# Sliding windows on one Trainium2 core: three DMA rings in place of two, other packet sizes, a last store in parts

## Chip, cores and metric

The kernel runs on one core of a Trainium2 chip. The metric is device time in microseconds; lower is better. The kernel before takes 763.64 us (median of three runs, 762.43 to 763.97).

## What is computed

For each of 32 batches of 4096 rows by 256 float32, the 127 windows of 64 rows that start every 32 rows are copied out:

```python
n_windows = (length - window_size) // stride + 1      # (4096 - 64) // 32 + 1 = 127
for i in range(n_windows):
    start = i * stride
    result[:, i] = x[:, start:start + window_size].copy()
```

Nothing is calculated. The input is 134 MB, the output 266 MB: each row, but for the first and last 32 of a batch, is written twice.

## The kernel before

Thirty-two rows of a batch are one block: 128 blocks of 32 KB in a batch. Window w is blocks w and w + 1, 64 KB, contiguous in input and output. There are two ways to make a batch's output.

A *copied* batch goes from HBM to HBM (`copy`, L93): 127 rows of 64 KB, in three DMAs of 80, 32 and 15 rows. `COPY_PARTS` (L16) gives in how many parts a row is cut, so the packets are 16, 32 and 16 KB. SP issues these DMAs. A DMA spreads its outermost rows evenly over up to 16 DMA engines; the 15-row DMA uses 15.

A *staged* batch is read once and written twice. `load` (L75) brings it to an SBUF tile, one block to each of the 128 partitions; `store` (L83) writes the tile to the output two times, shifted by half a window: `half` 0 makes block j the first half of window j, `half` -1 the second half of window j - 1. Both are issued by ACT in packets of 16 KB (`2 * BLOCK_PARTS`, so 65536 / 4 bytes). There is no window 127, and none before window 0, so a store also writes one block into the first half-window of the next batch and one into the last half-window of the batch before. Whatever writes those two batches must come later, or must be mended.

The 12 odd batches 1 to 23 are staged (`STAGED`), through five tiles (`BUFS`). The other 20 are copied. Their order is made by `_order` (L102): first the four batches of `EARLY`, 18, 20, 22 and 24, then batch 25, and then the batches 26 to 31 between those that touch a staged batch ("tied": 0, 2, ..., 16). Counted from 0, the tied batches stand at places 5, 6, 8, 10, 11, 13, 15, 16 and 18 of the 20, and each waits on SP for the stores of its staged neighbours (L134 to L137); the later of those is store 0 for batch 0, store 1 for batch 2, up to store 8 for batch 16. The `EARLY` batches don't wait: they are written before the stores of their neighbours (ACT waits for them once, L146), and the seven half-windows that those stores then spoil are written again at the end (L151 to L158) by small DMAs of 32 KB in 2 KB packets, each behind its store.

ACT's own order is load 0, load 1, store 0, load 2, store 1, and so on. A load into a tile that has been used waits for that tile's store (L79), a store waits for its load (L88). At the end SP waits for all stores and copies and clears the 12 semaphores one by one (L159 to L163).

All bytes thus go through two queues: q1, SP's, with 166.5 MB of copies, and q10, ACT's, with 50.3 MB of loads and 100.7 MB of stores. DMA engines take packets from the queues that have some.

Of the kernel before, what the change touches and what calls it, by code (L numbers as in the profile page):

```python
# [1 line left out]

# [4 lines left out]


STAGED = tuple(range(1, 24, 2))
BUFS = 5  # L10

EARLY = (18, 20, 22, 24)

BLOCK_PARTS = 2

COPY_PARTS = ((80, 4), (32, 2), (15, 4))  # L16


class _Geometry:


    def __init__(self, x, out, W, S):
        self.B, self.L, self.D = x.shape
        self.x, self.out = x, out
        self.n_win = (self.L - W) // S + 1
        self.n_blk = self.L // S
        self.blk = S * self.D
        self.win = W * self.D
        assert W == 2 * S and self.n_blk == self.n_win + 1 == 128

    def src(self, b, block, dims):

        at = (b * self.n_blk + block) * self.blk
        return bass.AP(self.x.tensor, self.x.offset + at, dims)

    def dst(self, b, half, dims):

        at = b * self.n_win * self.win + half * self.blk
        return bass.AP(self.out.tensor, self.out.offset + at, dims)

    def rows(self, b, w0, n):

        s, d = [[self.blk, n], [1, self.win]], [[self.win, n], [1, self.win]]
        return self.dst(b, 2 * w0, d), self.src(b, w0, s)

    def half(self, b, half, block):

        dims = [[self.blk // 16, 16], [1, self.blk // 16]]
        return self.dst(b, half, dims), self.src(b, block, dims)


class _Kernel:
    def __init__(self, nc, g, tiles):
        self.nc, self.g, self.tiles = nc, g, tiles
        self.loaded = [nc.alloc_semaphore(f"loaded{i}") for i in range(len(tiles))]
        self.stored = [nc.alloc_semaphore(f"stored{i}") for i in range(len(tiles))]
        self.copied = nc.alloc_semaphore("copied")
        self.early = nc.alloc_semaphore("early")
        self.count = {}

    def start(self, engine, out, in_, sem, parts=1):
        engine.dma_start(out=out, in_=in_, max_dma_last_dim=65536 // parts).then_inc(sem, 16)
        self.count[id(sem)] = self.count.get(id(sem), 0) + 16

    def all_of(self, engine, sem):
        engine.wait_ge(sem, self.count[id(sem)])

    def slot(self, n):
        return divmod(n, len(self.tiles))

    def after_store(self, engine, n):
        turn, i = self.slot(n)
        engine.wait_ge(self.stored[i], 32 * (turn + 1))

    def load(self, n):  # L75

        g, (_, i) = self.g, self.slot(n)
        if n >= len(self.tiles):
            self.after_store(self.nc.scalar, n - len(self.tiles))  # L79
        src = g.src(STAGED[n], 0, [[g.blk, g.n_blk], [1, g.blk]])  # L80
        self.start(self.nc.scalar, self.tiles[i][:, :], src, self.loaded[i], 2 * BLOCK_PARTS)

    def store(self, n):  # L83

        g, (turn, i) = self.g, self.slot(n)
        self.nc.scalar.wait_ge(self.loaded[i], 16 * (turn + 1))  # L88
        for half in (0, -1):
            dst = g.dst(STAGED[n], half, [[g.win, g.n_blk], [1, g.blk]])  # L90
            self.start(self.nc.scalar, dst, self.tiles[i][:, :], self.stored[i], 2 * BLOCK_PARTS)

    def copy(self, b, sem):  # L93

        w = 0
        for rows, parts in COPY_PARTS:
            self.start(self.nc.sync, *self.g.rows(b, w, rows), sem, parts)
            w += rows
        assert w == self.g.n_win


def _order(B):  # L102


    near = {b for s in STAGED for b in (s - 1, s + 1)}
    order = list(EARLY) + [b for b in range(B) if b not in near and b not in STAGED]
    tied = sorted(near - set(EARLY))
    n = len(order) + len(tied)
    for b in tied:
        behind = max(STAGED.index(s) for s in (b - 1, b + 1) if s in STAGED)  # L110
        order.insert(-(-(2 * behind + 5) * n // (2 * len(STAGED))), b)
    return order


@with_exitstack
def kernel(
    ctx: ExitStack,
    tc: tile.TileContext,
    x: bass.AP,
    window_size: bass.AP,  # L120
    stride: bass.AP,
    out: bass.AP,
):
    nc = tc.nc
    W, S = int(window_size), int(stride)
    g = _Geometry(x, out, W, S)
    assert 0 not in STAGED and g.B - 1 not in STAGED
    pool = ctx.enter_context(tc.tile_pool(name="blocks", bufs=1))
    tiles = [pool.tile([g.n_blk, g.blk], x.dtype, name=f"xb{i}") for i in range(BUFS)]

    with tc.tile_critical():
        k = _Kernel(nc, g, tiles)
        for b in _order(g.B):
            if b not in EARLY:  # L134
                for s in (b - 1, b + 1):
                    if s in STAGED:
                        k.after_store(nc.sync, STAGED.index(s))  # L137
            k.copy(b, k.early if b in EARLY else k.copied)
        k.load(0)
        waited = False  # L140
        last = len(STAGED) - 1
        for n, s in enumerate(STAGED):
            if n < last:
                k.load(n + 1)
            if not waited and (s - 1 in EARLY or s + 1 in EARLY):
                k.all_of(nc.scalar, k.early)  # L146
                waited = True
            k.store(n)


        k.all_of(nc.sync, k.early)  # L151
        for n, s in enumerate(STAGED):
            if s - 1 in EARLY or s + 1 in EARLY:
                k.after_store(nc.sync, n)
            if s - 1 in EARLY:
                k.start(nc.sync, *g.half(s - 1, 2 * g.n_win - 1, g.n_blk - 1), k.copied)
            if s + 1 in EARLY:
                k.start(nc.sync, *g.half(s + 1, 0, 0), k.copied)  # L158
        for n in range(len(STAGED)):  # L159
            k.after_store(nc.sync, n)  # L160
        k.all_of(nc.sync, k.copied)
        for sem in [*k.loaded, *k.stored, k.copied, k.early]:
            nc.sync.sem_clear(sem)  # L163


# [1 line left out]
_INS = ['x', 'window_size', 'stride']  # L167
_OUTS = [((32, 127, 64, 256), 'float32')]

_NUMBERS = {'window_size': 64, 'stride': 32}  # L170


# [26 lines left out]
```

## Time and profile before

| | |
|---|---|
| median of the runs | 763.64 us |
| the profiled execution | 768.4 us |
| its span, first to last instruction | 766.6 us |
| packets, bytes | 19837, 317.70 MB |
| mean rate | 414 GB/s |
| HBM read, written | 217.02 MB, 267.35 MB |
| first bulk packet, last packet | 2.0 us, 763.8 us |

The program has no compute instruction that matters (four memsets on GpSimd, 0.2 us), so the page's chain of waits and its groups of instructions say nothing. What is left to read is the DMA part: slices of the span with the DMA engines' busy share and their rate, the queues, the list of issues with the time from issue to landing, stretches of time with their rate, and what the queues' own sequencers waited for.

The list of issues has, for each kind, output and input, queue, count, KB each, and the median us from issue to landing:

```profile
out_dram<-in_x_dram SPq DMA_DIRECT2D x20, 5120.0 KB, 114.8
out_dram<-xb ACTq DMA_DIRECT2D x24, 4096.0 KB, 84.6
xb<-in_x_dram ACTq DMA_DIRECT2D x12, 4096.0 KB, 123.2
out_dram<-in_x_dram SPq DMA_DIRECT2D x20, 2048.0 KB, 116.7
out_dram<-in_x_dram SPq DMA_DIRECT2D x20, 960.0 KB, 97.7
out_dram<-in_x_dram SPq DMA_DIRECT2D x7, 32.0 KB, 48.3
```

The first, fourth and fifth rows are the three DMAs of a copy, the sixth the small ones at the end. A DMA lands some 100 us after its issue because it stands in its queue behind others. What SP's sequencer waited for (us in total, times, longest):

```profile
SPq L62 <- DMA out_dram<-xb: 61.2, 2, 40.2
SPq L73 <- DMA out_dram<-xb: 19.2, 3, 9.4
SPq L66 <- DMA out_dram<-in_x_dram: 7.7, 1, 7.7
```

The first two rows are waits for stores, the third is the wait at the end for the last copies. While SP waits, its queue still holds DMAs that were issued before.

### The profile page before, as it was taken

The numbers are of one execution on the slowest core, as the hardware profiler recorded it, in microseconds if no ns is written. First come the engines' busy times: TensorE is split into PE (matmuls) and PEld (weight loads), VectorE is DVE, ScalarE is ACT, GpSimd is POOL, SyncE is SP. The second block draws the span as 40 slices with busy tenths as digits, with TensorE's granted clock in tenths as the row PEclk, the third lists the DMA queues.
The fourth block names the chain that finished last, engine by engine and source line by source line (L and its number), as shares of the span: only waits on it lengthen the run. The fifth ranks groups of instructions, "written<-read, shape, count | busy, mean of one in ns | idle before, by whom it ended". The sixth has DMA issues, their size and how long they took to land. (4 is left out here: it accounts for less than half of the span.)

```text
span 766.6 us, 180 instructions
## 1 busy us (share of the span) xinstructions
POOL 0.2 (0%) x4
## 2 busy tenths in 40 slices
POOL 0000000000000000000000000000000000000000
DMA  8999999999999999999999999999999999999996
GB/s 371 425 410 421 405 428 431 408 411 427 423 415 421 431 415 425 432 408 416 427 420 417 431 420 420 423 428 410 414 427 419 422 428 418 417 428 421 420 406 237
DMA packets 19837, 317.70 MB, mean 414 GB/s; under 512 B 1628, under 2 KB 1628, under 8 KB 1740
## 3 DMA queue, kind: packets, MB, share of 16 engines
q1 hardware_dynamic: 10044, 166.70, 51.9%
q10 hardware_dynamic: 9792, 151.00, 47.3%
q14 instruction: 1, 0.01, 0.0%
HBM read 217.02 MB, written 267.35 MB: 632 GB/s over the span
## 5 line engine op out<-in xcount | busy, mean ns | idle before, releaser
L180 POOL MEMSET const-bfloat16-1.0<- 128x1 bf16 x1 | 0.1, 102 | 0.0
L180 POOL MEMSET const-uint8-127<- 128x1 uint8 x1 | 0.1, 102 | 0.0
L180 POOL MEMSET const-float32-0.0<- 128x1 f32 x1 | 0.1, 99 | 0.2 <-issue 0.2
L180 POOL MEMSET const-float32-1.0<- 128x1 f32 x1 | 0.1, 99 | 0.0
## 6 DMA issues: line engine op xcount, KB each, us to landing
out_dram<-in_x_dram SPq DMA_DIRECT2D x20, 5120.0 KB, 114.8
out_dram<-xb ACTq DMA_DIRECT2D x24, 4096.0 KB, 84.6
xb<-in_x_dram ACTq DMA_DIRECT2D x12, 4096.0 KB, 123.2
out_dram<-in_x_dram SPq DMA_DIRECT2D x20, 2048.0 KB, 116.7
out_dram<-in_x_dram SPq DMA_DIRECT2D x20, 960.0 KB, 97.7
out_dram<-in_x_dram SPq DMA_DIRECT2D x7, 32.0 KB, 48.3
```

What stands on the lines that cost most here:

```text
L180: nc = _bacc.Bacc("TRN2", target_bir_lowering=False, num_devices=1)
```

## The change

- Loads move from ACT to GpSimd and get packets of 8 KB, but for load 0, which stays on ACT, is issued first of all, and has packets of 32 KB and a semaphore of its own. GpSimd issues loads 1 to 11 one after the other, each waiting only for its tile.
- ACT then holds load 0 and the stores, which keep their 16 KB packets.
- A copy's three DMAs have 96, 16 and 15 rows, in packets of 32, 16 and 64 KB.
- The last store (batch 23) is made in three parts of 32, 32 and 64 partitions, each with both halves: first the two outer parts, with a semaphore of their own, then the middle one. The two small DMAs that mend batches 22 and 24 wait for the outer parts alone.
- At the end GpSimd instead of SP waits for all semaphores, resets its DMA queue and clears the semaphores as one range.

The order of the copies, the staged batches, the five tiles and the bytes moved are the same.

```diff
-BLOCK_PARTS = 2
-
-COPY_PARTS = ((80, 4), (32, 2), (15, 4))
+
+LOAD_PACKET = 8192
+STORE_PACKET = 16384
+COPIES = ((96, 2), (16, 4), (15, 1))
+
+
+LAST = ((0, 32), (96, 32), (32, 64))
...
-    def start(self, engine, out, in_, sem, parts=1):
-        engine.dma_start(out=out, in_=in_, max_dma_last_dim=65536 // parts).then_inc(sem, 16)
+    def start(self, engine, out, in_, sem, packet=65536):
+        engine.dma_start(out=out, in_=in_, max_dma_last_dim=packet).then_inc(sem, 16)
...
         if n >= len(self.tiles):
-            self.after_store(self.nc.scalar, n - len(self.tiles))
+            self.after_store(self.nc.gpsimd, n - len(self.tiles))
         src = g.src(STAGED[n], 0, [[g.blk, g.n_blk], [1, g.blk]])
-        self.start(self.nc.scalar, self.tiles[i][:, :], src, self.loaded[i], 2 * BLOCK_PARTS)
-
-    def store(self, n):
+        if n == 0:
+            self.start(self.nc.scalar, self.tiles[i][:, :], src, self.first)
+        else:
+            self.start(self.nc.gpsimd, self.tiles[i][:, :], src, self.loaded[i], LOAD_PACKET)
+
+    def store(self, n, p0, rows, sem=None):
...
         g, (turn, i) = self.g, self.slot(n)
-        self.nc.scalar.wait_ge(self.loaded[i], 16 * (turn + 1))
+        if n == 0:
+            self.all_of(self.nc.scalar, self.first)
+        else:
+            self.nc.scalar.wait_ge(self.loaded[i], 16 * (turn + (i > 0)))
         for half in (0, -1):
-            dst = g.dst(STAGED[n], half, [[g.win, g.n_blk], [1, g.blk]])
-            self.start(self.nc.scalar, dst, self.tiles[i][:, :], self.stored[i], 2 * BLOCK_PARTS)
+            dst = g.dst(STAGED[n], 2 * p0 + half, [[g.win, rows], [1, g.blk]])
+            src = self.tiles[i][p0 : p0 + rows, :]
+            self.start(self.nc.scalar, dst, src, sem or self.stored[i], STORE_PACKET)
...
         w = 0
-        for rows, parts in COPY_PARTS:
-            self.start(self.nc.sync, *self.g.rows(b, w, rows), sem, parts)
-            w += rows
+        for n, parts in COPIES:
+            self.start(self.nc.sync, *self.g.rows(b, w, n), sem, 4 * self.g.win // parts)
+            w += n
...
         k = _Kernel(nc, g, tiles)
+        k.load(0)
         for b in _order(g.B):
...
-        k.load(0)
+        for n in range(1, len(STAGED)):
+            k.load(n)
...
-            if n < last:
-                k.load(n + 1)
             if not waited and (s - 1 in EARLY or s + 1 in EARLY):
                 k.all_of(nc.scalar, k.early)
                 waited = True
-            k.store(n)
+            if n < last:
+                k.store(n, 0, g.n_blk)
+            else:
+                for p0, rows in LAST:
+                    alone = p0 > 0 and p0 + rows < g.n_blk
+                    k.store(n, p0, rows, None if alone else k.fringe)
...
-            if s - 1 in EARLY or s + 1 in EARLY:
+            if n == last:
+                k.all_of(nc.sync, k.fringe)
+            elif s - 1 in EARLY or s + 1 in EARLY:
                 k.after_store(nc.sync, n)
...
-        for n in range(len(STAGED)):
-            k.after_store(nc.sync, n)
-        k.all_of(nc.sync, k.copied)
-        for sem in [*k.loaded, *k.stored, k.copied, k.early]:
-            nc.sync.sem_clear(sem)
+
+        sems = [*k.loaded, *k.stored, k.first, k.early, k.copied, k.fringe]
+        for sem in sems:
+            k.all_of(nc.gpsimd, sem)
+        nc.gpsimd.dma_reset()
+        used = sorted(sem.num for sem in sems)
+        assert used == list(range(used[0], used[-1] + 1))
+        nc.gpsimd.sem_clear(range(used[0], used[-1] + 1))
```

## The prediction

> **What bounds the kernel now.** I read the slices of the span first, then the queues, then stretches of the trace chosen by what the queues carry. From the page, the DMA engines' share, the rate and the queues:
>
> ```profile
> DMA  8999999999999999999999999999999999999996
> GB/s 371 425 410 421 405 428 431 408 411 427 423 415 421 431 415 425 432 408 416 427 420 417 431 420 420 423 428 410 414 427 419 422 428 418 417 428 421 420 406 237
> ...
> q1 hardware_dynamic: 10044, 166.70, 51.9%
> q10 hardware_dynamic: 9792, 151.00, 47.3%
> ```
>
> The 16 DMA engines are busy from the second slice to the last but one; the two queues (q1 is SP's, q10 ACT's) fill 99.2% of them. So no wait and no instruction bounds the kernel: bytes, packets and slow packets do. The packet records give the prices: a 2 KB packet takes 84 ns, 16 KB 611, 32 KB 1213 (medians). These lie on one line, 9 ns plus 602 ns for each 16 KB. Off it I read 310 ns for 8 KB and 2417 for 64 KB; no packet of these queues has those sizes.
>
> Next, stretches (columns: stretch and length in us, POOL busy, clock, DMA share, GB/s). First ACT stores beside SP copies, all in 16 KB; then stores beside 32 KB copies; then ACT loads beside copies:
>
> ```profile
> 237.00:250.00 13.00, 0.00 (x0) 1.00 1.02 436
> 426.00:447.00 21.00, 0.00 (x0) 1.00 1.00 428
> 549.00:561.00 12.00, 0.00 (x0) 1.00 1.00 430
> ...
> 69.00:75.00 6.00, 0.00 (x0) 1.00 0.97 399
> 372.00:381.00 9.00, 0.00 (x0) 1.00 1.00 421
> 675.00:685.00 10.00, 0.00 (x0) 1.00 1.02 433
> ...
> 146.00:166.00 20.00, 0.00 (x0) 1.00 1.00 406
> 336.00:354.00 18.00, 0.00 (x0) 1.00 0.99 403
> 398.00:418.00 20.00, 0.00 (x0) 1.00 1.02 423
> ```
>
> Over all such stretches (11, 10 and 10 of them; 168, 77 and 192 us) the weighted means are 428.9, 424.0 and 415.8 GB/s. Without a slow packet 16 KB packets would give 16 x 16384 B / 611 ns = 429.0, and alternate 32 and 16 KB packets 16 x 49152 / 1824 = 431.2. So the loss is 0% with stores, 1.7% with stores beside 32 KB copies, 3.2% with loads. A copy reads and writes HBM, a load only reads, a store only writes: HBM is read by 50, 67 and 100% of the moved bytes. The loss follows this share.
>
> Last, how the whole adds up and how it ends:
>
> ```profile
> 0.00:20.00 20.00, 0.20 (x4) 1.00 0.91 376
> 20.00:720.00 700.00, 0.00 (x0) 1.00 1.01 421
> 720.00:746.00 26.00, 0.00 (x0) 1.00 0.94 403
> 746.00:754.00 8.00, 0.00 (x0) 1.00 0.97 395
> 754.00:767.00 13.00, 0.00 (x0) 1.00 0.42 152
> ```
>
> A 15-row copy uses 15 engines, so the sixteenth has 20 x 64 KB less, 48 us, and is done near 720: the share falls to 15/16. For each of the other 15, copies take 20 x (24 x 611 + 4 x 1213) = 390.3 us, loads 12 x 16 x 611 = 117.3, stores 24 x 16 x 611 = 234.6, small packets some 1.5: 743.7 us. Packets ran from 2.0 to 763.8, 761.8 us; 18.1 us are lost. The rows place them: 20 to 720 us at 421 against 429.4 (mix of both prices) is 13.7; about 0.6 in the start; 0.2 before 754; after 754 the rest, 152 x 13 = 1.98 MB, is 4.9 us of work at 402.6 (15 engines) in the 9.8 us to 763.8, so 4.9. That is 19.4, near enough. The 2.8 us behind 763.8 are a landing (SP's wait ends at 764.86), 12 clears of 0.06 us and the program's end.
>
> **The change part by part.** *Packets.* Copies become 20 x (12 x 1213 + 4 x 611 + 2417) = 388.3 us per engine, 2.0 less. Load 0 is 8 packets of 32 KB, 9.7; the other 11 are 32 packets of 8 KB each, 11 x 32 x 310 = 109.1; together 118.8, 1.5 more. Stores are unchanged. Sum: -0.5 us.
>
> *Three rings.* The packet records show one packet from each queue in turn: both in 16 KB, each moved 1.06 MB in 45 to 50 us; with SP in 32 KB, 1.57 against 0.57 MB from 30 to 35. With three, a turn is one packet of each. A copy is 17 packets, so SP needs 340 turns. A load and a store are 32 packets each, so they advance together: load n lands at turn 32n, store n starts at turn 9 + 32n (behind load 0, 8 turns, and one for landing and issue). The load is 8 turns early, 16 us at 388.3/340 + 0.611 + 0.310 = 2.06 us per turn; load landings spread over at most 8.7 us (354.3 to 363.0), so this covers them. SP's waits: copy number p is served from turn 17p, and the store it waits for is done at turn 41 + 32k. The closest is p = 16 behind store 7: 272 against 265, 14 us. GpSimd's waits have 87 turns. Queued behind a late store would be SP's next copies; their ring would run dry, while ACT's and GpSimd's kept the engines busy. Hence the order costs nothing.
>
> *What the engines lose.* The three-ring stage is 388.3 + 340 x 0.921 + 4.8 (load 0's packets are larger) = 706 us. In a turn group 512 KB are copied, 272 stored, 136 loaded: in 70.4% of the bytes HBM is read. The nearest row is 67%, 1.7%: 12.0 us. The ends are 0 (the store row) and 22.6 (the load row, 3.2%). Then SP is done with 12 load and 53 store packets per engine left: 36 us, first mixed, then stores alone, without loss by the store row. Start 0.6 as before.
>
> *The end.* Before, the last packets are SP's copies alone; after, stores. Their 4.9 us are spread between engines plus 0.7 of slow packets (records 750 to 760); I keep 4.2, with bounds 1.7 and 4.5 (slowest landing less the mean of 15, in store 0 and in store 11). The half-block copies wait for the two outer parts of the last store; the middle part, 16 packets per engine, 9.8 us, hides them: before, they took from 755.27 to the end of the packets. Without this cover they cost at least issue, 1.1 us to a first packet and a landing of 1.1, some 3 us.
>
> *Closing.* 11 of 12 clears go, -0.66; the queue reset isn't in the trace: bounds 0 and 0.18 (GpSimd's drain at the start); I take 0.16. Sum -0.5.
>
> *Sum.* Lost: 12.0 + 0.6 + 4.2 = 16.8 for 19.4, so -2.6; with -0.5 and -0.5, **-3.6 us**: span 763.0 for 766.6. The profiled execution took 768.4 and the runs 763.64 in the median; I take the same difference off the median: 760.0.
>
> The rows above show that which streams share an engine moves its rate, 428.9 to 415.8 with the same two queues. The Trainium skill, "DMA: Bandwidth & Descriptors", section "Rules for kernel authors", speaks against this change: spreading DMAs over SP, ACT and GpSimd gives no bandwidth, since all share the same 16 engines. By it only packets and closing would remain, -1.0 us.
>
> *GpSimd's packets.* No packet generated by GpSimd is in the trace. The cheap end is 301 ns (the line without its 9), the dear end the runtime's own 8 KB packets on queue 14, median 531 ns (seven of them). Each ns over 310 costs 352 packets x 1 ns = 0.35 us: -3 to +78 us. I take the line, since it fits three sizes on the same engines, while queue 14 loads instructions. The same page, section "Measured (HBM→SBUF, 128 partitions, SWDGE, issued from GpSimd)", gives 425 GB/s for 16 MB; as an estimate this is 308 ns for 8 KB, and the sum stays; no run here shows it.
>
> **Rivals.** *Dearer packets from GpSimd (slower).* Place: each of 352 turns. It decides from 10 ns over the line (3.5 us) and makes the kernel slower from about 15; at half of the dear end, 110 ns, it is +39, near 799. For it: the only 8 KB packets seen are 1.7 times the line. Against: they belong to another queue. *Loads never pause (slower).* If a load beside copies costs the load row's loss whatever its rate, 22.6 for 12.0: 760.0 + 10.6 = 770.6. For it: every load stretch is slow but the last few only slightly. Against: loads move a seventh of a turn instead of half. *Loads thinned out cost nothing (much faster).* 760.0 - 12.0 = 748. For it: the loss is 0 at 50%. Against: 1.7% at 67%. *Only the order moves (no change).* The loss stays with the bytes read, whenever they are: packets and closing alone, -0.5 - 0.5, give 762.6. It is also the time if GpSimd's ring isn't served one for one: stores then wait for loads and copies take the turns, but no engine idles. For it: every byte is still moved by the same 16 engines. Against: the rate follows the mix.
>
> **How the numbers follow.** A measurement here tells 0.2% (1.5 us) from no change. Forecast 0.38, own range 757 to 762; much faster 0.18; no change 0.16; loads never pause 0.10; dearer packets 0.18. Faster 0.56, same 0.16, slower 0.28. The range runs from 746 (no loss, spread 1.7) to 771 (the load row's loss); dearer packets mostly lie beyond.
>
> **What would show it.** Right: 8 KB packets near 310 ns, some 423 GB/s from 20 to 700 us, SP's bulk packets ending near 725 us, stores ending last. Wrong: 8 KB packets well over 320 ns, a rate at or under 421, ACT idle for loads, or SP's half-block copies landing last.

## The result and the profile after

The changed kernel takes 756.58 us (median, 756.12 to 758.48) beside 763.5 for the kernel before (761.43 to 764.13): a ratio of 0.9918, 95% interval 0.9902 to 0.9934, 6.9 us less. When both were measured again later, beside the experiments, the ratio was 0.9979 (0.9967 to 0.9992), 766.24 for 767.28. The gain has its sign both times; its size is not a constant, and what sets it was not found.

The profiled execution of the changed kernel took 756.54 us, its span is 754.8 us for 766.6. Of these 11.8 us some 4.9 belong to the profiled execution of before, 768.4 us. It lies over all six runs that were measured beside the changed kernel (761.43 to 764.13) and within those of the later repetition (765.65 to 769.61), while the one of the changed kernel lies on its median. So the two traces overstate the change: they show of what kind it is, and not how much of the 6.9 us.

From the page of the changed kernel, DMA share and rate by slice, and the queues, now three (q0 is GpSimd's):

```profile
DMA  9999999999999999999999999999999999999996
GB/s 369 405 429 427 432 425 431 426 435 423 439 410 439 422 427 436 425 435 416 439 422 429 425 425 424 427 428 426 429 430 430 431 421 428 424 430 422 414 404 279
...
q1 hardware_dynamic: 6584, 166.70, 51.7%
q10 hardware_dynamic: 6736, 104.86, 32.8%
q0 software_dynamic: 5808, 46.14, 14.8%
```

The engines are as full as before, and the same bytes pass in a shorter span: six of the 40 slices lie under 415 GB/s, where ten did. The same reading in stretches (stretch and length in us, POOL busy, clock, DMA share, GB/s), first the kernel before, then the changed one:

```profile
20.00:700.00 680.00, 0.00 (x0) 1.00 1.01 421
...
20.00:700.00 680.00, 5.18 (x7) 1.00 1.01 427
700.00:720.00 20.00, 0.00 (x0) 1.00 0.98 412
720.00:741.00 21.00, 0.00 (x0) 1.00 0.93 391
741.00:755.00 14.00, 0.00 (x0) 1.00 0.60 252
```

Between these two executions, what fell is the time of slow packets. Summed over all packet records, what a packet took above the price of its size (84, 310, 611, 1213 and 2417 ns for 2, 8, 16, 32 and 64 KB) is 19.3 us per engine before and 9.1 after; in the records from 20 to 700 us alone 17.3 and 7.3. The last packet ended at 763.8 and now at 752.6, 11.2 us earlier: the 10.2 us of slow packets, 0.5 of packet prices, and little else. Mean times: copies of 32 KB 1253 ns before, 1228 after; ACT's 16 KB 628 before (loads and stores), 616 after (stores); GpSimd's 8 KB packets 317, median 309.

What the sequencers waited for in the changed kernel, GpSimd first (its group, with its idle time), then SP's queue:

```profile
L68 POOL DMA_DIRECT2D xb<-in_x_dram x11 | 8.3, 753 | 462.5 <-DMA out_dram<-xb 461.5
...
SPq L79 <- DMA out_dram<-xb: 365.4, 8, 59.5
SPq L68 <- DMA out_dram<-xb: 136.3, 4, 54.6
```

GpSimd issues a load in 0.75 us and waits for tiles, and SP waits 501.7 us for stores where it waited 80.4. Neither costs anything: the packet records show q1 at work in every 10 us up to the end of its bulk at 740.5. A wait in a queue's sequencer says nothing while that queue still holds DMAs.

### The profile page after: what moved, and what is told of

Same layout as the page of the kernel before. It is cut to its first block, busy times and chain, and to the rows that moved or that the text cites. A ratio compares the mean times of both kernels' runs of the same rounds, so it can differ in the third digit from the quotient of the medians.

```text
span 754.8 us, 177 instructions
## 1 busy us (share of the span) xinstructions
POOL 8.5 (1%) x15
## 4 chain that ended last, share of the span: by engine, by line
another core or an unknown queue 61%; POOL 1%; issue 0%; PEldq 0%
POOL xb L68 1%; PEldq L217 0%
## 5 line engine op out<-in xcount | busy, mean ns | idle before, releaser
L68 POOL DMA_DIRECT2D xb<-in_x_dram x11 | 8.3, 753 | 462.5 <-DMA out_dram<-xb 461.5
```

The source lines that it names most:

```text
L68: engine.dma_start(out=out, in_=in_, max_dma_last_dim=packet).then_inc(sem, 16)
```

## The experiments

Two theories stood at first. THINNING: loads in bursts beside copies make packets slow, and spreading them over the whole time cures it. THIRD RING: the third ring itself hides slow packets. From the first results came COPY SHARE: a copied byte is both read from and written to HBM, and packets get slow where copies have too large a part of the moved bytes. Each ratio is to the kernel before, measured beside it on the same chip.

**Copies' packets undone.**

```diff
-COPIES = ((96, 2), (16, 4), (15, 1))
+COPIES = ((80, 4), (32, 2), (15, 4))
```

> The changed kernel with one part undone: the copies' DMAs are cut as before, 80, 32 and 15 rows in packets of 16, 32 and 16 KB; three rings stay. Two theories of where the 6.9 us come from. THINNING: the loss per engine depends on how much of the moved bytes reads HBM at a time, and the change gains by spreading loads thinly over the whole time. THIRD RING: a third ring by itself hides slow packets, whatever it carries. In turns of one packet per ring, a copy now takes 28 packets and 3 semaphore packets, 20 copies 620 turns; stores and loads need some 34 turns each, 12 stores about 420. So loads and stores end with a third of the copies left, and SP's copies then run alone. THINNING: a stretch of copies alone at the end, with the loss of the copies-only stretch of the kernel before (10 to 14% from 750 to 760 us), over 100 us or more; total near 764 to 770. THIRD RING: the loss is low while three rings run, at most the ratio of the two packet sizes counts, total 757 to 760.

786.47 us, ratio 1.0256 (1.0243 to 1.0269): slower than expected by either. Stretches with three rings, then with copies alone:

```profile
40.00:540.00 500.00, 5.18 (x7) 1.00 1.01 431
640.00:740.00 100.00, 0.00 (x0) 1.00 0.99 327
```

With copies at some 42% of the bytes the engines lose nothing for 500 us. But loads and stores are through at 630 us, and the copies left over run alone at 327 GB/s, 24% under the 429 that 16 KB packets give. The packet sizes decide who gets what share of a turn, and so whether anything is left alone at the end.

**Third ring undone.**

```diff
+            if n < last:
+                k.load(n + 1)          # on ACT, in 16 KB
-            self.start(self.nc.gpsimd, ..., LOAD_PACKET)
+            self.start(self.nc.scalar, ..., STORE_PACKET)
```

> The changed kernel with the other part undone: loads go back to ACT in 16 KB, load n + 1 ahead of store n as before; copies in 32, 16 and 64 KB stay, and the rest too. THINNING: loads come in bursts again, beside copies that now have two thirds of the bytes, so the loss is that of the kernel before or more: 761 to 766. THIRD RING: the gain is gone as well, near 763. If the copies' larger packets alone made the gain (a third theory, SIZES), the time stays at 756 to 758.

799.94 us, ratio 1.0421 (1.0401 to 1.0441), far over what any of the three theories expected. The gain isn't the larger packets alone. From the stretches:

```profile
20.00:260.00 240.00, 0.00 (x0) 1.00 1.00 402
...
740.00:760.00 20.00, 0.00 (x0) 1.00 1.00 408
760.00:780.00 20.00, 0.00 (x0) 1.00 0.98 281
```

Packets of 32 and 16 KB give copies 63% of the bytes here (253 of 402 GB/s in the packet records), and the rate is 402 where such packets allow 431. The copies are through at 731 us, and ACT runs on alone until 796. The last row is a surprise: stores alone, most of them in parts of 32 partitions, move 281 GB/s, where whole stores moved 408 just before. Their packets are slow: from 760 to 775 a 16 KB packet took 923 to 970 ns (means of 5 us) for 611.

**Loads in 32 KB on GpSimd.**

```diff
-LOAD_PACKET = 8192
+LOAD_PACKET = 32768
```

> The changed kernel with GpSimd's loads in packets of 32 KB in place of 8 KB: three rings, but a load now takes four times the bytes of a turn, so loads come in bursts (4 : 2 : 4 while one runs, 80% of the bytes read HBM) and GpSimd then waits for a tile. THINNING: the loss returns in the bursts, 759 to 765. THIRD RING: nothing changes, 756 to 757.5.

776.62 us, ratio 1.0129 (1.0116 to 1.0142), again over both expectations. The stretches speak against both theories:

```profile
60.00:100.00 40.00, 0.00 (x0) 1.00 1.00 432
...
160.00:180.00 20.00, 0.47 (x1) 1.00 0.98 401
...
540.00:740.00 200.00, 0.00 (x0) 1.00 1.00 407
```

In the first a load takes its four parts of ten: HBM is read by 80% of the bytes, and nothing is lost, so THINNING is wrong as put. In the others GpSimd waits for a tile or has no load left; copies have 62% beside stores, and the rate falls to 401 and 407. The loss comes not where loads burst but where they pause.

**Loads spread in two rings, by quarters of 32 partitions.** In the kernel before, ACT issues behind each quarter of store n a quarter of load n + 2.

```diff
-            k.store(n)
+            for q in range(4):
+                k.store(n, q)
+                if n + 2 <= last:
+                    k.load(n + 2, q)
```

> The kernel before, two rings and all packet sizes as they were, but with loads spread out on ACT's ring: loads and stores are cut into quarters of 32 partitions, and behind each quarter of store n stands one quarter of load n + 2 (4 MB of loads in 12 MB of ACT's packets, instead of one block of load behind two of store). THINNING: the read share is near 67% all the time, the gain of the changed kernel appears without a third ring, 755 to 759. THIRD RING: no gain, 762 to 765.

804.13 us, ratio 1.0479 (1.0446 to 1.0511), over both expectations. This tells the theories apart badly, since pieces of 32 partitions are slow here even with nothing beside them; near the end, where ACT's stores are alone and a 16 KB packet took 822 to 1091 ns (means of 5 us):

```profile
760.00:780.00 20.00, 0.00 (x0) 1.00 0.83 238
```

**The same by columns,** all 128 partitions in each DMA: store half, half load, store half, half load.

```diff
+            for q in range(2):
+                k.store(n, q)          # half = -q
+                if n + 2 <= last:
+                    k.load(n + 2, q)   # columns q * blk / 2 and on
```

> The kernel before with loads spread on ACT's ring, this time cut by columns: each load in two DMAs of 128 partitions by 16 KB, one behind each half of a store (store n first half, load n + 2 left half, second half, right half). Packets are the 16 KB of before, all 128 partitions take part in each DMA. Theories as they stand after the first four runs. THINNING: read share near 67% all the time, 755 to 759. COPY SHARE (the engines lose only where copies, which read and write HBM, are over about half of the moved bytes; 0 at 40 to 43%, some 1% at 57%, 5 to 8% at 67%, 22% for copies alone): here copies stay at half as before and loads still run beside them, so nearly nothing changes, 760 to 766.

779.17 us, ratio 1.0153 (1.0139 to 1.0166). THINNING falls: in two rings spread loads gain nothing. COPY SHARE missed too, since it expected no change; why this order costs 12 us more is open.

**Copies in 64 KB, three rings.**

```diff
-COPIES = ((96, 2), (16, 4), (15, 1))
+COPIES = ((96, 1), (16, 1), (15, 1))
```

> The changed kernel with all copies in 64 KB packets: three rings run, 8 : 2 : 1, so copies have 73% of the bytes while all have work. THIRD RING: no more loss than in the changed kernel (427 GB/s from 20 to 700 us where all three run). COPY SHARE: HBM moves 1.73 bytes for each byte, and the total of reads and writes seen so far never passed some 670 GB/s, so 385 to 390 GB/s in these stretches, 9 to 10% lost; total over 775.

816.87 us, ratio 1.0642 (1.0629 to 1.0656).

```profile
40.00:180.00 140.00, 0.74 (x1) 1.00 1.00 391
```

As COPY SHARE had it, 391 GB/s, 9% under the 431.9 of these packets. THIRD RING falls: with three rings at work and copies at 67% of the bytes (262 of 391 GB/s; 73% in a turn of bulk packets alone), the loss is larger than the 7% of two rings.

**Copies in 8 KB, two rings.**

```diff
-COPY_PARTS = ((80, 4), (32, 2), (15, 4))
+COPY_PARTS = ((80, 8), (32, 8), (15, 8))
```

> The kernel before, two rings, with all copies in 8 KB packets, so that copies have a third of the bytes beside ACT's 16 KB. What makes a load beside copies slow? If it is the reads (all moved bytes read HBM in these stretches, here as before), the load stretches still lose 3% or more. If it is the sum of reads and writes (1.33 for each byte in place of 1.5), they lose nothing, as in the three-ring stretches of the kernel with 32 KB loads. The whole kernel gets slow, since copies alone are left at the end: ACT's 151 MB are done after some 530 us, and 91 MB of copies remain at 325 GB/s or less, 280 us; total 800 to 840.

822.5 us, one run. Loads beside copies, stores beside copies, copies alone:

```profile
152.00:165.00 13.00, 0.00 (x0) 1.00 1.01 427
170.00:196.00 26.00, 0.00 (x0) 1.00 1.01 430
...
560.00:780.00 220.00, 0.00 (x0) 1.00 0.99 328
```

Ten load stretches (111 us) give 428.5 in the mean; alternate 16 and 8 KB packets would give 426.9. All of the bytes read HBM, as in the load stretches of the kernel before, which lost 3.2%; with copies at a third instead of half, nothing is lost. So in this one run it isn't reading HBM with every byte that costs; what differs is the copies' part, and with it their packet size. That this is the sum of reads and writes is not shown: loads beside copies lost 3% before at a sum of 631 GB/s, and stores beside copies nothing at 648 (the table below).

**The last store whole,** and beside it the changed kernel again.

```diff
-LAST = ((0, 32), (96, 32), (32, 64))
+LAST = ((0, 128),)
```

> The changed kernel with the last store in one piece; the two small DMAs that mend batches 22 and 24 then wait for all of it. By the prediction's step the parts hide these small DMAs, and without them they cost some 3 us: 2 to 4 us over the changed kernel, 758.5 to 760.5 on the chip where that one takes 756.6. If something else covers them, no difference.

767.78 us, ratio 1.0007 (0.9996 to 1.0018), on a chip where the changed kernel had not been run: not to be read against 0.9918. Hence both, side by side:

> The changed kernel itself, unchanged, as the control for the runs beside it: the kernel before took 763.5 us where the changed one was first measured and 766 to 767 in the later calls, so times of different calls can't be set side by side. If the gain holds elsewhere, its ratio to the kernel before is again near 0.992 (0.989 to 0.995).

> The changed kernel with the last store in one piece, now beside the changed kernel itself. Its first trace ends with the two small DMAs landing 3 us behind the last store. So 2.5 to 3.5 us over the changed kernel of this call (ratio to it 1.003 to 1.005). If the ratio of 1.0007 in the call before was the parts alone, it would be 6 to 7 us.

The changed kernel 766.24 us, ratio 0.9979 (0.9967 to 0.9992): the expectation missed. With the last store whole 768.83, ratio 1.0015 (1.0000 to 1.0029), so the parts are worth 2.6 us. In the trace with the whole store the small DMAs are issued at 764.7 us and the last packet ends at 767.3, 2.9 behind the stores' last; in the changed kernel they are through at 758.0, 3.4 before it. The middle of this trace, and of that of the changed kernel beside it:

```profile
20.00:700.00 680.00, 5.18 (x7) 1.00 1.01 421
...
20.00:700.00 680.00, 5.18 (x7) 1.00 1.01 423
```

This changes what the gain of 6.9 us can be put down to. On these two chips the three rings and the packet sizes, without the parts of the last store, gained nothing over the kernel before (1.0007 and 1.0015). What is left of the gain in the repetition goes with the parts.

**No 64 KB packets.**

```diff
-COPIES = ((96, 2), (16, 4), (15, 1))
+COPIES = ((112, 2), (15, 4))
```

> The changed kernel with a copy in two DMAs: 112 rows in 32 KB and 15 rows in 16 KB, in place of 96, 16 and 15 in 32, 16 and 64 KB. Turns per copy stay 20 (14 + 1 and 4 + 1), packet time too (19426 for 19417 ns), but no 64 KB packets, in whose turns copies have 73% of the bytes. COPY SHARE: slightly less loss, 0 to 2 us under the changed kernel of this call. If 64 KB packets cost nothing (their mean was 2419 ns for 2417 off the line): no difference.

768.96 us, ratio 1.0030 (1.0015 to 1.0045), 2.7 over the changed kernel beside it. A miss: the slow-packet sum is 19.9 us per engine for 16.4. In the changed kernel beside it a 64 KB packet cost just its price, 2418 ns. That 14 packets of 32 KB in a row are worse than 12 is only a guess.

**A sixteenth engine for the 15-row copies.** For the 16 even batches, one window of all of them in one DMA, 15 times.

```diff
+            dst = bass.AP(..., [[2 * g.n_win * g.win, 16], [1, g.win]])
+            src = bass.AP(..., [[2 * g.n_blk * g.blk, 16], [1, g.win]])
```

> The changed kernel with the 15-row copies of the 16 even batches replaced: one window of all 16 even batches in one DMA, 16 rows for 16 engines, 15 such DMAs, one behind each of the first 15 copies; they touch no window that a store spoils. The four odd copied batches keep their 15 rows. Bytes and packets are the same, but the sixteenth engine, idle from about 716 us, now takes 15 of the 20 x 64 KB it lacked. Each of the other 15 has one packet of 64 KB less, 2.4 us. Expected 2 to 3 us under the changed kernel, if 16 engines 8 MB apart in the input are not slower than 15 engines 32 KB apart; slower than the changed kernel if they are.

783.27 us, ratio 1.0219 (1.0195 to 1.0244).

```profile
20.00:700.00 680.00, 5.19 (x7) 1.00 1.01 413
```

The 2.4 us of balance are lost many times over: 64 KB packets now take 2835 ns in the mean and up to 4349, for 2418, and packets of the other rings get slower beside them. The 16 engines read addresses 8 MB apart. The Trainium skill, "DMA: Bandwidth & Descriptors", section "Latency and other measured facts", tells of DMA copies that fall to half the rate at row pitches of 4 and 8 MiB; this run agrees in its direction (2835 for 2418 ns), and doesn't show the cause. No version here beats the changed kernel.

## Why the prediction was right, and where it was off

*Direction.* Forecast 760.0 and faster; measured 756.58, and in the repetition 1.0 us faster than the kernel before. The gain was to come mostly from fewer slow packets. The two traces of the first measurement show them, 19.3 and 9.1 us per engine, but that of before is of the execution of 768.4 us; the changed kernel's trace in the repetition has 16.4, and no trace of before was taken beside it. So the direction came out, the kind of the gain is likely, and how much of it slow packets make is open.

*The mis-sized term* is the loss of the three-ring stage. I took 1.7% of 706 us, 12.0 us, from the row of 32 KB copies beside stores. Read as the prediction reads it, from the rate, 427 from 20 to 700 us is 0.7% under the 430 of these packets, some 5 us, so 12.0 was too large by 7. The sum as a whole says the same: between first and last packet, 750.7 us, 743.2 are work, so 7.5 were lost where I added up 16.8. In the repetition the rate was 423, which is 11 to 12 us, and the loss as a whole 16.2. (The packet records give 7.3 and 13.8; they lie higher, for the kernel before too, 17.3 for some 13 by the rate.) So the term was wrong by more than half in the first measurement and right in the second, and the forecast of -3.6 lies between -6.9 and -1.0.

The kernel before moved less: 763.5, then 766.4 and 767.3. That the changed kernel works closer to where packets get slow, and so feels more of whatever differs, is a guess; what differs wasn't found.

*The reason behind the term* was half right, and its size partly luck. I ordered the rows by the share of bytes that read HBM, and read 67% for the row it came from. The packet records give copies 60% of the bytes there, in stretches of 5 to 12 us; other stretches at 62 and 63%, 200 us and longer, lose 6 and 7%. With what the runs add, ordered by copies' share of the moved bytes (rates and shares summed from the packet records of the stretches, so a point or two off the rows above; "lost" against undisturbed packets):

| stretch | copies' share | GB/s | lost | HBM read + written, GB/s |
|---|---|---|---|---|
| copies_8k, loads beside | 32% | 428 | 0 | 567 |
| load_32k, loads and stores beside | 38% | 433 | 0 | 596 |
| old_copies, loads and stores beside | 42% | 431 | 0 | 612 |
| before, stores beside | 50% | 431 | 0 | 648 |
| before, loads beside | 52% | 416 | 3% | 631 |
| after, 20 to 700 us | 53% | 427 | 0.7% | 653 |
| changed_again, 20 to 700 us | 53% | 423 | 2% | 647 |
| before, stores beside 32 KB copies | 60% | 423 | 2% | 676 |
| load_32k, stores beside | 62% | 406 | 6% | 660 |
| two_rings, 20 to 260 us | 63% | 402 | 7% | 655 |
| copies_64k, 40 to 180 us | 67% | 391 | 9% | 653 |
| old_copies, copies alone | 100% | 328 | 24% | 655 |

The last column is the rate times one plus the share. In the four stretches from 62% up, 100 to 240 us long, it stands at 653 to 660 whatever the engines could move, which looks like a limit on reads plus writes. It isn't proved to be one: in the short stretches with 32 KB copies 676 passed, and at 53% full engines would give only 430 x 1.53 = 658, so those rows can't tell. Nor is the sum all: loads beside copies lose at 631, stores don't at 648. This, thin_cols with 633 and the repetition with 647 no run explains.

What the runs do show is that long stretches with copies at 62% and over lose 6 to 24%. The bytes of the kernel are fixed, 166.7 of 317.7 MB or 52% copied, so a stretch with fewer copies is paid for by another with more, as in old_copies and load_32k. The step from there to the gain is argued: before, SP's 32 KB copies raised the share and bursts of loads took turns with stores, 640 GB/s of reads and writes from 20 to 700 us; the change keeps all three kinds flowing and ends its rings nearly together, 653, and in the repetition 647.

*Packets.* 8 KB: 310 ns off the line, median 309 measured; 64 KB: 2417 and 2418. The rival of dearer packets from GpSimd is dead. The estimate from the Trainium skill's page "DMA: Bandwidth & Descriptors", section "Measured (HBM→SBUF, 128 partitions, SWDGE, issued from GpSimd)", 308, agrees. Its rule in "Rules for kernel authors", that a third queue gives no bandwidth, fits copies_64k (391 GB/s with three queues) and nearly fits the repetition (423, and 421 with the last store whole); the first pair of traces, 421 and 427, would speak against it if they were of like executions.

*Turns.* Wrong by the semaphores. A DMA ends with a packet of 4 bytes on each engine, 9 ns, and that takes a turn of its own. The packet records of the changed kernel show it: from 100 to 600 us each engine, in the mean, took 270.7 packets from GpSimd's ring, 271.0 from SP's and 270.6 from ACT's, but 262.7, 230.5 and 254.6 if those of 4 bytes are left out. (From 30 to 35 us of the kernel before, which I had read as one for one, it was 48 against 35.) So a copy is 20 turns, not 17, and a turn 1.89 us (388.3 / 400 + 0.921), not 2.06. A load of 33 turns is then 62 us, where I had put 66. Measured are 61.4 (ACT issues store 1 at 72.8 and store 10 at 625.3, each when its load lands). SP's bulk ended at 740.5, not near 725. It hardly moved the time: no ring ran dry, and loads stayed ahead, load 1 landing 18.8 us before store 0.

*The end.* Hiding the small DMAs was priced at some 3 us, measured 2.6. Closing was priced at -0.5: from the last packet to the end of the span it was 2.86 us and is 2.15, so -0.7.

*The base.* I put the median 3 us under the span, as it was before. But the profiled execution of before lay 4.9 us over its median; that of the changed kernel lay on its own, and its span is 1.8 us under it. On spans the gain looks like 11.8 us, on medians it is 6.9: the sum is to be made on one, and judged on the other.

*Rivals.* Loads thinned out cost nothing, 748: the loss of 0.7% lies more than halfway to it, but thin loads as such are not the cause. Loads never pause: the opposite is what is dear (load_32k), and in old_copies loads that never paused cost nothing for 500 us. Only the order moves, -1.0 us: in the first measurement the gain was 6.9. The repetition, with 1.0 and a rate of 423 in the middle for 421, does not rule this rival out.

## What to carry to other kernels

Where DMA engines are full and bytes are fixed, look at stretches by what the queues carry and compare each rate with that of undisturbed packets; here the loss stood in certain mixes. Packet sizes set the shares of queues that take turns. Choose them such that no stretch is left with far more copies than the mean, and all queues end together; here versions that strayed from this were 10 to 55 us slower than the kernel before, while keeping to it gained 1 to 7, part of it by the parts of the last store. Count the semaphore packets as turns. Repeat a gain under 1% beside the old kernel before building on it, and take the traces that are to explain it from the same measurement.

## What was not expected of the hardware

Copies from HBM to HBM alone moved 327 to 328 GB/s, in 16 and in 8 KB packets, so 654 GB/s of reads and writes, while the same engines move 429 with stores beside them. Stores mostly in pieces of 32 partitions, with nothing beside them, ran at 238 and 281 GB/s, whole ones at 408. A 9 ns semaphore packet takes as much of the order as one of 64 KB (270.7, 271.0 and 270.6 packets from three rings). GpSimd's 8 KB packets cost the same as the line through those of SP and ACT.
